# Two places of a two-layer decoder kernel in another order: the end of the linear recurrence, and the casts, sums and first products at the entries of the FFNs

## The chip, the core and the metric

The kernel runs on one core of a Trainium2 chip. The metric is device microseconds (us) of one execution, as a median over several. Three runs of the kernel before gave 2107.00, 2108.28 and 2108.45 us. A core has five engines that run side by side and wait for each other through semaphores: PE (matrix products), ACT (ScalarE), DVE (VectorE), POOL (GpSimd) and SP, whose queue issues most DMAs. PEld is PE's loading of weights. PE writes its sums to PSUM, in banks of 128 partitions by 512 floats; all else lies in SBUF.

## The reference

A decoder trunk of two layers on 1024 tokens of width 1024. Layer 0 mixes tokens by a linear recurrence with 8 heads of 128, layer 1 by attention over a sliding window of 128. Each mixer and each FFN is followed by a layer norm of alpha times the residual plus the result.

```python
q, f, i, g = jnp.split(h @ w_in, 4, axis=-1)
fg = lb + (1.0 - lb) * jax.nn.sigmoid(heads(f))
o = hgrn2_chunkwise(jax.nn.silu(heads(q)), 1.0 - fg, heads(i), jnp.log(fg))
#   S_t = diag(f_t) S_{t-1} + k_t v_t^T ; o_t = S_t^T q_t
o = o * lax.rsqrt(jnp.mean(jnp.square(o), -1, keepdims=True) + RMS_EPS)
o = o * g_norm_w * jax.nn.silu(heads(g))
mix = o.reshape(B, S, D) @ w_out

h = layer_norm(ALPHA * h + mix, ln_mix_g, ln_mix_b)
u = causal_depthwise_conv3(h @ w_in) + conv_b      # 1024 -> 2 x 2816
a, b = jnp.split(u, 2, axis=-1)
h = layer_norm(ALPHA * h + (jax.nn.silu(a) * b) @ w_out, ln_ffn_g, ln_ffn_b)
```

## The kernel before

**Numbers.** All is fp32. An operand of a product is kept as two parts: a high part, which ACT makes by a cast, and a low part, which DVE makes by subtracting the high part from the source (`split`, L197 and L249). A product then takes three matmuls, high by high (L222), high by low (L223) and low by high (L224), all written by `mm3`. `T` is the input of products, transposed, both parts; `HL` holds weights.

**Order.** The object `od` keeps a model clock: each matmul adds its time to `od.t`, and after each group of three `od.tick()` lets the generators whose time has come issue their next work on ACT and DVE. A generator's `yield 2.0` means that its next part is issued when PE's model clock is 2 us on. In the recurrence the instructions of all engines stand in exactly the order in which they were issued; in the FFN only PE's do, and a scheduler orders ACT and DVE by tiles and priority (`urgent()`). Each engine runs its own instructions in order, so one that waits holds up those behind it.

**The recurrence and its end.** The four projections (q and f as one pair for each head, i and g as another) are made by seven products p = 1 to 7 on half-size blocks (sums of blocks of the input in `Y`, `T` and `TX`), 98 steps n in the list `line`. They go to four banks of PSUM. `evacuate` empties a bank after its last product: by a copy (L1391, p = 1; L1393, L1395, L1397) or, for f (p = 4), by a tanh of the late half, after `yield 2.0` a tanh of the early half (L1403), and then `kept_back` (L1023 and L1024: the affine step for fg, and kp = 1 - fg). Beside the projections `recur` runs the recurrence of each head: products qs x kp (L1136) and qp = qs x fg (L1137), a tree over levels of block length, transposes of kp, then the state chain, St copied from the first PSUM part (L1210) and six steps (L1212). The last head, 7, is finished after the projections. The output projection (L1550, `out_pass`) covers it: `out_split` makes the parts of its weights (cast L1453, low part queued in `out_lows`), and `move` brings the normed outputs of heads 0 to 6, which were stored in HBM and come back by DMA into the tiles fg, qs, kp and Y, into `T` (cast L1470, low part queued in `moved_lows`); head 6 comes from `VG`. Head 7's output is normed in L1247 to L1266: sums of squares (sq), og, eight transposes of og (L232), gates (L1265, in four pieces), cast and low part into `T`, and it enters the last products (kc = 7).

**The entry of the FFN.** `Up` makes the first FFN product, again as seven products p on sums of blocks. `ln` takes one block of 128 rows through the layer norm (L280, L283), eight transposes on PE, and the parts. Blocks 4 to 7 are done first; for blocks tb = 0 to 3 it writes the parts of `T` and a copy `hf` of the transposed block (L437), from which, with `sf` of block tb + 4, DVE makes three sums (L447 to L449), whose parts go to `T2` (p = 7) and `TX` (p = 6 and 3). `run` first makes products 4 and 5, on blocks 4 to 7 alone, while blocks 0 to 3 are made; then 1 and 2, which read blocks 0 to 3, each with 512 columns; then 6, 7 and 3, which read the sums. `fc` is the piece of 128 outputs; `collect` takes a product out of PSUM (p = 1: two copies on ACT, L510 and L511). Products 6 use the banks of products 1 again.

Of the kernel before, what the change touches and what calls it, by code (L numbers as in the profile page):

```python
# [10 lines left out]
F32 = mybir.dt.float32  # L11
# [123 lines left out]
def trunk(ctx: ExitStack, tc: tile.TileContext, a: dict, out: bass.AP):  # L135
# [270 lines left out]
    class Up:  # L406
        def __init__(self, l, pool, rx):
            self.l, self.rx = l, rx
            self.wv = a["ffn_w_in"][l].rearrange("(kc p) c -> p kc c", p=P)
            self.TX = pool.tile([P, 2, 2, 4, 512], F32R, name="TX")  # L410
            self.T2 = pool.tile([P, 2, 4, 512], F32R, name="T2")
            self.left = None if l else pool.tile([P, 512], F32, name="lf")
            self.W, self.raw, self.pieces = {}, {}, 0

        def row_loads(self):

# [5 lines left out]
        def ln(self, tb):  # L422
            with urgent():
                ln_affine(tb, self.rows, lambda hs: ynd[:, tb, hs], 2 if tb == 3 else 1)
            yield 10.0 if tb >= 4 and self.l else 8.0 if self.l else 13.0 if tb >= 4 else 11.0
            turned = lambda t: (self.rx[2 * t - 4] if t in (2, 3) else Y[:, t, :]).rearrange("p (k t) -> p k t", k=KC)
            hf = turned(tb)
            ts = slice(tb * P, (tb + 1) * P)
            with urgent():
                for q in range(2):  # L430
                    ps, ks = psmm(), slice(4 * q, 4 * q + 4)
                    for k in range(4):
                        tr(ps[:, k * P:(k + 1) * P], Y[:, tb, (4 * q + k) * P:(4 * q + k + 1) * P])
                    pv = ps.rearrange("p (k t) -> p k t", k=4)
                    if tb < 4:
                        split(T[:, 0, ks, ts], T[:, 1, ks, ts], pv)
                        nc.scalar.copy(hf[:, ks], pv)  # L437
                    elif q == 0:
                        nc.scalar.copy(hf[:, ks], pv)
                    else:  # L440
                        split(T[:, 0, ks, ts], T[:, 1, ks, ts], pv)
                        tt(hf[:, ks], hf[:, :4], pv, op=add)
                        split(T[:, 0, :4, ts], T[:, 1, :4, ts], hf[:, ks])
                        return
            sf = turned(tb + 4)
            a11, a12, a21, s1 = hf[:, :4], hf[:, 4:], sf[:, :4], sf[:, 4:]
            tt(a21, a11, a21, op=sub)  # L447
            tt(a11, s1, a11, op=sub)
            tt(a12, a12, a11, op=sub)  # L449
            split(self.T2[:, 0, :, ts], self.T2[:, 1, :, ts], a21)  # L450
            yield 100.0
            pair = hf.rearrange("p (c k) t -> p c k t", c=2)
            split(self.TX[:, :, 0, :, ts], self.TX[:, :, 1, :, ts], pair)

        def weights(self, fc):
            self.weight_load(fc)
# [31 lines left out]
            split(blocks(1, 0), blocks(1, 1), r1)  # L488
            split(blocks(2, 0), blocks(2, 1), r2)

        def product(self, p, fc, ps):
            TX = self.TX
            moving = {1: lambda j, k: T[:, j, k, :512], 2: lambda j, k: T[:, j, 4 + k, :512],
                      3: lambda j, k: TX[:, 1, j, k, :], 4: lambda j, k: T[:, j, 4 + k, 512:],
                      5: lambda j, k: T[:, j, k, 512:], 6: lambda j, k: TX[:, 0, j, k, :],
                      7: lambda j, k: self.T2[:, j, k, :]}[p]
            block = {1: 0, 2: 1, 5: 2, 4: 3, 7: 4, 6: 5, 3: 6}[p]
            ws = self.W[fc]
            fixed = lambda j, k: (ws[6][:, 512 * j + 128 * k:512 * j + 128 * k + 128] if block == 6 else
                                  ws[block // 2 * 2 + j][:, 512 * (block % 2) + 128 * k:512 * (block % 2) + 128 * k + 128])  # L500
            for k in range(4):
                mm3(ps, lambda j: fixed(j, k), lambda j: moving(j, k), k == 0, k == 3)
                od.tick()
            return ps

# [51 lines left out]
        def run(self, ready, down):  # L557

            od.finish(ready[:4])
            tiles = [psax(), psax()]  # L560
            ax = [tiles[i % 2][:, i // 2 * 512:(i // 2 + 1) * 512] for i in range(4)]

            for (p, fc), ps in zip([(p, fc) for p in (4, 5) for fc in range(2)], ax):
                self.product(p, fc, ps)
            od.finish(ready[4:])
            mm = [psmm() for _ in range(4)]
            self.pairs = [mm, ax]
            for (p, fc), ps in zip([(p, fc) for p in (1, 2) for fc in range(2)], mm):
                self.collect(p, fc, self.product(p, fc, ps))
            for fc in range(2):  # L570
                self.collect(6, fc, self.product(6, fc, mm[fc]))
            for fc in range(2):
                self.collect(7, fc, self.product(7, fc, mm[2 + fc]))
                self.collect(4, fc, ax[fc])
                self.collect(5, fc, ax[2 + fc])
            self.weights(2)
            for fc in range(2):
                self.collect(3, fc, self.product(3, fc, mm[fc]))
            banks, n = mm[2:] + ax[:2] + mm[:2] + ax[2:], 0
            for fc in range(2, NF):  # L580
                if fc > 2:
                    self.weights(fc)
                for p in (1, 2, 6, 7, 4, 5, 3):
                    self.collect(p, fc, self.product(p, fc, banks[n % 8]))
                    n += 1
                    if fc == NF - 1 and p in (1, 6, 4):
                        down.ahead.append(down.operands(0, len(down.ahead)))
# [140 lines left out]
    with tc.tile_pool(name="t", bufs=1, reuse_waits="tile") as raws, hgrn_pool as hp:  # L728
# [323 lines left out]
        def recur(h, qs, fg, kp):  # L1052
# [80 lines left out]

            yield 0.0
            r0 = hp.tile([P, S], F32, name="St")
            nc.vector.tensor_tensor(r0, qs, kp, op=ALU.mult)  # L1136
            nc.vector.tensor_tensor(qp, qs, fg, op=ALU.mult)  # L1137
            od.vec(4.4)
            r1 = hp.tile([P, S // 2], F32, name="r1")
            nc.vector.tensor_tensor(r1, kp[:, 0::2], qp[:, 1::2], op=ALU.mult)  # L1140
            update(0)
            r2 = hp.tile([P, 2, S // 4, 2], F32, name="kd")
            for j in range(2):
                nc.vector.tensor_tensor(r2[:, j], kp[:, j::4].unsqueeze(2).to_broadcast([P, S // 4, 2]),
# [235 lines left out]
        def evacuate(m, p, ps, taken):  # L1380
# [9 lines left out]
            if p == 1:  # L1390
                nc.scalar.copy(first[:, early], ps)  # L1391
            elif p == 6:
                nc.scalar.copy(second[:, early], ps)  # L1393
            elif p == 5:
                nc.scalar.copy(second[:, late], ps)  # L1395
            elif p == 4 and g:
                nc.scalar.copy(first[:, late], ps)  # L1397
                od.spawn(turn_values(h), 3.0)
            elif p == 4:
                nc.scalar.activation(first[:, late], ps, AF.Tanh, scale=0.5)  # L1400
                taken.append(1)
                yield 2.0
                nc.scalar.activation(first[:, early], first[:, early], AF.Tanh, scale=0.5)  # L1403
                kept_back(h, first, kp, slice(0, S))
            else:
                half, to = {2: (early, first), 7: (late, second), 3: (early, second)}[p]
                tt(to[:, half], to[:, half], ps, op=add)
                od.vec(0.7)
                taken.append(1)
                yield od.behind(0.1, 0.8)  # L1410
                if p != 2:
                    nc.scalar.activation(to[:, half], to[:, half], AF.Silu)
# [38 lines left out]
        def out_split(u, place):  # L1451
# [4 lines left out]
            def low():  # L1456
                low_part(hl[:, 1], oraw[u], hl[:, 0], None)
                od.vec(1.2)
                if u == 0:
                    out_load(3)  # L1460
            out_lows.append((od.t + 1.3, low))
            yield 0.0

        def move(h0, n, half, src, wait):
# [18 lines left out]
        with tc.manual_schedule(engines={EN.PE, EN.SP, EN.Activation, EN.DVE, EN.Pool}):  # L1483
# [26 lines left out]
            for n, (m, p) in enumerate(line):  # L1510
# [2 lines left out]
                product(n)  # L1513
                opened[0] = len(line)
                h, g = pairs[m]
                if n == 90:
                    od.finish(evacs[12])
                    ready.append((NH - 1, targets[12]))
                elif n > lead and line[n - lead][1] == 4 and pairs[line[n - lead][0]][1] == 0 and n - lead < 90:
                    mr = line[n - lead][0]  # L1520
                    od.finish(evacs[mr])
                    ready.append((pairs[mr][0], targets[mr]))
                if n == 90:
                    ensure(len(line) - 1)
                if n in (91, 93, 95, 97):
                    u = (91, 93, 95, 97).index(n)
                    moved.append(od.spawn(out_split(u, (1, 2, 3, 0)[u]), 4.0 if u == 0 else 0.4))
                if n == 93:
                    Y.renew(0)
                    kept = [hp.tile([P, S], F32, name=name, bufs=b) for name, b in (("fg", 1), ("qs", 1), ("kp", 2))]  # L1530
                    halves = [[stage(t, (2 * i, 2 * i + 1), 0) for i, t in enumerate(kept)],
                              [stage(Y[:, i, :], (2 * i, 2 * i + 1), 1) for i in range(3)]]
                    moved += [od.spawn(move(2 * i, 2, 0, halves[0][i], 6.0 + 2.0 * i)) for i in range(3)]
                if n == 94:
                    moved += [od.spawn(move(2 * i, 2, 1, halves[1][i], 9.0 + 2.0 * i)) for i in range(2)]
                if n == 95:
# [392 lines left out]
```

## Time and profile before

The profiled execution took 2106.06 us; its span, from the first to the last instruction, is 2104.3 us, and all times in the views count from the span's start.

| what | value |
|---|---|
| median of three runs | 2108.28 us |
| profiled execution | 2106.06 us |
| its span | 2104.3 us |
| ACT busy in the span | 972.7 us |
| DMA, mean over the span | 136 GB/s |
| recurrence and its output projection end at about | 480 us |
| first FFN entry (products 4, 5, then 1) | 523 to 552 us |
| second FFN entry | 1466 to 1490 us |

In a row of the timeline stand start, length, engine, line, operation, output and inputs by the program's names without buffer numbers, shape and count; in brackets the idle time just ahead of it and the instruction that ended it. A matmul of 512 columns has a length of 0.39, but those that follow each other overlap in part; a row with x8 runs from the start of the first to the end of the last.

### The profile page before, as it was taken

Reading aid. Unit: us, or ns where it says so; the run is one execution under the profiler, and the core shown is the slowest. Engines: PE = TensorE matmul, PEld = TensorE weight load, DVE = VectorE, ACT = ScalarE, POOL = GpSimd, SP = SyncE. Lnnn points to the kernel's source line nnn. Section 1 sums busy time; section 2 is a strip of 40 time slices with the busy share of each in tenths; the row PEclk is TensorE's granted clock in tenths of the full one; section 3 lists DMA queues with packets and bytes.
Section 4 is the critical chain, followed back from the end, with each engine's and each line's share of the span. In section 5 each row is a group of like instructions: output and inputs, shape, how many; then the busy total and the mean of one; then the engine's idle time right before and its main releaser. Section 6 shows DMA issues by size and latency. Waiting matters only on the chain.

```text
span 2104.3 us, 31586 instructions
## 1 busy us (share of the span) xinstructions
PE 2081.6 (99%) x12303; PEld 1734.4 (82%) x12303; DVE 1775.6 (84%) x2424; ACT 972.7 (46%) x1580; POOL 176.3 (8%) x210
## 2 busy tenths in 40 slices
PE   9999999999999999999999999999999999999998
PEld 8878888778788888888888888888888888888886
DVE  6778887769999998987987678979999998978986
ACT  6555555643544444444433367733544444444430
POOL 1000000001000000000001123412000000000002
PEclk9999999999999999999999999999999999999999
DMA  4111111333256866538755411051266776459662
GB/s 154 41 51 51 51 52 51 119 118 120 84 147 176 193 163 156 136 124 299 247 184 171 140 36 46 14 174 78 87 177 171 170 190 150 116 163 323 220 217 94
DMA packets 239823, 286.82 MB, mean 136 GB/s; under 512 B 30216, under 2 KB 160440, under 8 KB 239416
## 3 DMA queue, kind: packets, MB, share of 16 engines
q1 hardware_dynamic: 223360, 238.26, 35.0%
q0 software_dynamic: 15456, 46.16, 11.0%
q8 instruction: 97, 1.59, 0.3%
q14 instruction: 54, 0.44, 0.1%
q10 hardware_dynamic: 856, 0.37, 0.1%
HBM read 241.72 MB, written 89.15 MB: 157 GB/s over the span
## 4 chain that ended last, share of the span: by engine, by line
PE 88%; DVE 7%; ACT 3%; DMA 1%; issue 1%; POOL 0%; SPq 0%; DVEq 0%; ACTq 0%; POOLq 0%
PE psmm L222 17%; PE psmm L224 17%; PE psmm L223 17%; PE psax L222 9%; PE psax L224 9%; PE psax L223 9%; PE psax L228 3%; PE psmm L228 1%; PE psax L1703 1%; PE psmm L232 1%; PE psax L232 1%; DVE HL L197 1%; DVE T L197 1%; PE psmm L1550 1%; ACT HL L1310 1%
## 5 line engine op out<-in xcount | busy, mean ns | idle before, releaser
L222 PE MATMUL psmm<-T,HL 128*128 128x512 f32 x816 | 322.5, 395 | 3.5 <-ACT T L249 2.2
L223 PE MATMUL psmm<-T,HL 128*128 128x512 f32 x816 | 318.0, 390 | 1.4 <-DVE T L197 1.4
L224 PE MATMUL psmm<-T,HL 128*128 128x512 f32 x816 | 318.1, 390 | 0.2 <-DVE HL L197 0.2
L532 DVE SCALAR_TENSOR_TENSOR Y<-Y,cwt,Y 128x1023 f32<-128x1023 f32 (+1 forms) x176 | 225.2, 1281 | 45.5 <-ACT Y L530 44.1
L249 ACT CAST HL<-rx 128x1024 fp32r<-128x1024 f32 (+1 forms) x151 | 151.4, 1007 | 184.5 <-DMA rx<-in_ffn_w_in_dram 48.5
L197 DVE TENSOR_TENSOR HL<-rx,HL 128x1024 fp32r<-128x1024 f32 (+1 forms) x151 | 174.6, 1161 | 20.9 <-ACT HL L249 20.8
L222 PEld LDWEIGHTS psmm<-T,HL 128*128 128x128 f32 x816 | 153.3, 188 | 36.0 <-ACT T L249 2.4
L224 PEld LDWEIGHTS psmm<-T,HL 128*128 128x128 f32 x816 | 153.2, 188 | 33.0 <-DVE HL L197 0.6
L223 PEld LDWEIGHTS psmm<-T,HL 128*128 128x128 f32 x816 | 153.2, 188 | 32.2 <-DVE T L197 2.1
L222 PE MATMUL psax<-T,HL 128*128 128x512 f32 x392 | 152.7, 390 | 0.0
L224 PE MATMUL psax<-T,HL 128*128 128x512 f32 x392 | 152.5, 389 | 0.0
L223 PE MATMUL psax<-T,HL 128*128 128x512 f32 x392 | 152.5, 389 | 0.0
L530 ACT ACTIVATE Y<-Y,cwt 128x1024 f32<-128x1024 f32 x88 | 108.8, 1238 | 91.7 <-DVE Y L519 86.3
L197 DVE TENSOR_TENSOR HL<-raw,HL 128x512 fp32r<-128x512 f32 (+1 forms) x121 | 92.2, 787 | 31.9 <-ACT HL L1310 22.5
L271 POOL TENSOR_TENSOR rs<-rs,nhalf 128x1 f32<-128x1 f32 x32 | 45.6, 1427 | 735.3 <-DVE rs L270 735.3
L249 ACT CAST HT<-rx 128x1024 fp32r<-128x1024 f32 (+1 forms) x37 | 35.5, 960 | 112.5 <-DVE rx L486 60.3
L222 PE MATMUL psmm<-HL 128*128 128x512 f32 x220 | 86.8, 394 | 0.0
L223 PEld LDWEIGHTS psax<-T,HL 128*128 128x128 f32 x392 | 73.7, 188 | 15.3
L222 PEld LDWEIGHTS psax<-T,HL 128*128 128x128 f32 x392 | 73.5, 188 | 15.3
L224 PEld LDWEIGHTS psax<-T,HL 128*128 128x128 f32 x392 | 73.6, 188 | 15.2
L224 PE MATMUL psmm<-HL 128*128 128x512 f32 x220 | 85.8, 390 | 0.0
L223 PE MATMUL psmm<-HL 128*128 128x512 f32 x220 | 85.6, 389 | 0.0
(406 smaller groups left out, 5177.3 us busy)
## 6 DMA issues: line engine op xcount, KB each, us to landing
rx<-in_ffn_w_in_dram SPq DMA_DIRECT2D x136, 256.0 KB
rx<-gd SPq DMA_DIRECT2D x118, 256.0 KB
bsd<-in_ffn_w_out_dram POOLq DMA_DIRECT2D x36, 768.0 KB, 8.6
gd<-Y SPq DMA_DIRECT2D x44, 512.0 KB
raw<-in_hgrn_w_in_dram SPq DMA_DIRECT2D x30, 512.0 KB
rx<-in_ffn_w_out_dram SPq DMA_DIRECT2D x54, 256.0 KB
R<-bsd SPq DMA_DIRECT2D x44, 256.0 KB
Y<-in_ffn_w_in_dram SPq DMA_DIRECT2D x40, 256.0 KB
```

The source lines that it names most:

```text
L197: make = lambda e: e.tensor_tensor(lo, src, hi.bitcast(F32), op=ALU.subtract)
L222: nc.tensor.matmul(ps, st(0), mv(0), start=start, stop=False, skip_group_check=onto)
L223: nc.tensor.matmul(ps, st(0), mv(1), start=False, stop=False, skip_group_check=onto)
L224: nc.tensor.matmul(ps, st(1), mv(0), start=False, stop=stop, skip_group_check=onto)
L228: nc.tensor.matmul(ps, lhsT, rhs, start=start, stop=stop, **kw)
L232: nc.tensor.transpose(ps, src, ident)
L249: nc.scalar.copy(hi, src)
L271: nc.gpsimd.tensor_tensor(rs, rs, nhalf, op=ALU.pow)
L530: nc.scalar.activation(c, u, AF.Identity, bias=cwt[:, l, 3, ci:ci + 1], scale=cwt[:, l, 2, ci:ci + 1])
L532: nc.vector.scalar_tensor_tensor(c[:, sh:], u[:, :S - sh], cwt[:, l, 2 - sh, ci:ci + 1], c[:, sh:], op0=ALU.mult, op1=ALU.add)
L1310: nc.scalar.copy(home(n)[:, 0], source(m, p))
L1550: nc.tensor.matmul(ps, T[:, x, kc, tb * P:(tb + 1) * P], us[kc][:, w, :], start=start and kc == 0, stop=False)
```

## The change

1. `evacuate`, p = 4: the early tanh, the affine step and kp are issued at 3.0 instead of 2.0 on the model clock.
2. `recur`: qp is made ahead of qs x kp; in head 7 another 3.0 lies between the first update and the products for `kd`.
3. Main loop: head 7's gates are finished and handed to `recur` at n = 91, not 90. The tiles for the moved heads are loaded in the order kp, qs, fg (heads 0 and 1 into kp), and their moves start at 3.0, 5.0 and 7.0, not 6.0, 8.0 and 10.0. The low part of the first output weights may go 6.0 behind its cast, not 1.3.
4. `Up.ln`, both layers: high part and copy are made by ACT one after the other, and the low part is made from the copy. The three sums are made as s1 - a11, a11 - a21 and a12 - s1, and each sum's parts directly behind it, in the order of the products that read them (6, 7, 3). The generator stops after the parts of `T` and after each sum; `make` takes all blocks to a given stage.
5. `Up.run`: blocks 0 to 3 are taken to stage 1 ahead of products 1, to stages 2, 3 and 4 behind. In layer 0 products 1 are made in two goes, 24 matmuls on the columns of blocks 0 to 2 (384), and 24 on those of block 3 (128).

```diff
@@ Up.ln
                     if tb < 4:
-                        split(T[:, 0, ks, ts], T[:, 1, ks, ts], pv)
+                        nc.scalar.copy(T[:, 0, ks, ts], pv)
                         nc.scalar.copy(hf[:, ks], pv)
+                        low_part(T[:, 1, ks, ts], hf[:, ks], T[:, 0, ks, ts], None)
...
+            self.made[tb] = 1
+            yield 100.0
             sf = turned(tb + 4)
             a11, a12, a21, s1 = hf[:, :4], hf[:, 4:], sf[:, :4], sf[:, 4:]
+            tt(s1, s1, a11, op=sub)
+            split(self.TX[:, 0, 0, :, ts], self.TX[:, 0, 1, :, ts], s1)
+            self.made[tb] = 2
+            yield 100.0
             tt(a21, a11, a21, op=sub)
-            tt(a11, s1, a11, op=sub)
-            tt(a12, a12, a11, op=sub)
             split(self.T2[:, 0, :, ts], self.T2[:, 1, :, ts], a21)
+            self.made[tb] = 3
             yield 100.0
-            pair = hf.rearrange("p (c k) t -> p c k t", c=2)
-            split(self.TX[:, :, 0, :, ts], self.TX[:, :, 1, :, ts], pair)
+            tt(a12, a12, s1, op=sub)
+            split(self.TX[:, 1, 0, :, ts], self.TX[:, 1, 1, :, ts], a12)
+            self.made[tb] = 4
+
+        def make(self, ready, part):
+            for tb, task in enumerate(ready):
+                while self.made[tb] < part:
+                    od.step(task)
@@ Up.product: a slice cols of the columns, all 512 by default
-                mm3(ps, lambda j: fixed(j, k), lambda j: moving(j, k), k == 0, k == 3)
+                mm3(ps[:, cols], lambda j: fixed(j, k), lambda j: moving(j, k)[:, cols], k == 0, k == 3, n=cols.stop - cols.start)
@@ Up.run
-            od.finish(ready[4:])
+            self.make(ready[4:], 1)
...
-            for (p, fc), ps in zip([(p, fc) for p in (1, 2) for fc in range(2)], mm):
+            firsts = list(zip([(p, fc) for p in (1, 2) for fc in range(2)], mm))
+            if self.l == 0:
+                for (p, fc), ps in firsts[:2]:
+                    self.product(p, fc, ps, slice(0, 3 * P))
+            for part in range(2, 5):
+                self.make(ready[4:], part)
+            if self.l == 0:
+                for (p, fc), ps in firsts[:2]:
+                    self.collect(p, fc, self.product(p, fc, ps, slice(3 * P, 4 * P)))
+                firsts = firsts[2:]
+            for (p, fc), ps in firsts:
                 self.collect(p, fc, self.product(p, fc, ps))
@@ recur
             r0 = hp.tile([P, S], F32, name="St")
+            nc.vector.tensor_tensor(qp, qs, fg, op=ALU.mult)
             nc.vector.tensor_tensor(r0, qs, kp, op=ALU.mult)
-            nc.vector.tensor_tensor(qp, qs, fg, op=ALU.mult)
...
             update(0)
+            if h == NH - 1:
+                yield 3.0
             r2 = hp.tile([P, 2, S // 4, 2], F32, name="kd")
@@ evacuate, p == 4
-                yield 2.0
+                yield 3.0
@@ out_split
-            out_lows.append((od.t + 1.3, low))
+            out_lows.append((od.t + (6.0 if u == 0 else 1.3), low))
@@ main loop
-                if n == 90:
+                if n == 91:
                     od.finish(evacs[12])
                     ready.append((NH - 1, targets[12]))
...
-                if n == 90:
+                if n == 91:
                     ensure(len(line) - 1)
...
-                    kept = [... for name, b in (("fg", 1), ("qs", 1), ("kp", 2))]
+                    kept = [... for name, b in (("kp", 2), ("qs", 1), ("fg", 1))]
...
-                    moved += [od.spawn(move(2 * i, 2, 0, halves[0][i], 6.0 + 2.0 * i)) for i in range(3)]
+                    moved += [od.spawn(move(2 * i, 2, 0, halves[0][i], 3.0 + 2.0 * i)) for i in range(3)]
```

Lines of the changed kernel are 20 to 24 higher than those of the same code before.

**ACT at the last gates of the recurrence** (steps n = 91 to 93; fg, kp are head 7's, sq, ss belong to head 6, VG and raw to the next evacuation and the weights). Before:

```order
L1400 ACTIVATE fg<-psmm 128x512
L1310 CAST HL<-raw_112 128x512
L1403 ACTIVATE fg<-fg 128x512
L1023 ACTIVATE fg<-fg,lbt 128x1024
L1024 ACTIVATE kp<-fg,one 128x1024
L1310 CAST HL<-raw_113 128x512 x2
L1310 CAST HL<-raw_112 128x512
L1247 ACTIVATE sq,ss<-psax 128x128 x4
L1391 COPY VG_4157<-psmm 128x512
```

Now:

```order
L1424 ACTIVATE fg<-psmm 128x512
L1334 CAST HL<-raw_112 128x512
L1271 ACTIVATE sq,ss<-psax 128x128 x4
L1334 CAST HL<-raw_113 128x512 x2
L1334 CAST HL<-raw_112 128x512
L1415 COPY VG_4133<-psmm 128x512
L1427 ACTIVATE fg<-fg 128x512
L1045 ACTIVATE fg<-fg,lbt 128x1024
L1046 ACTIVATE kp<-fg,one 128x1024
```

The copy out of PSUM has moved ahead of the early tanh, the affine step and kp.

**DVE at the last chain of the recurrence** (low parts of output weights and of moved heads, then head 7's state chain; `VG_3489` is head 6). Before:

```order
L197 TENSOR_TENSOR HL<-raw_113,HL 128x1024
L197 TENSOR_TENSOR HL<-raw_114,HL 128x1024
L197 TENSOR_TENSOR T<-fg,T 128x2x512
L197 TENSOR_TENSOR T<-VG_3489,T 128x512
L197 TENSOR_TENSOR T<-qs,T 128x2x512
L197 TENSOR_TENSOR T<-kp,T 128x2x512
L1210 COPY St<-psax 128x128
L1212 SCALAR_TENSOR_TENSOR St<-St,tot,psax 128x128 x6
```

Now:

```order
L197 TENSOR_TENSOR HL<-raw_114,HL 128x1024
L197 TENSOR_TENSOR T<-kp,T 128x2x512
L197 TENSOR_TENSOR T<-qs,T 128x2x512
L197 TENSOR_TENSOR T<-fg,T 128x2x512
L1234 COPY St<-psax 128x128
L1236 SCALAR_TENSOR_TENSOR St<-St,tot,psax 128x128 x6
L197 TENSOR_TENSOR T<-VG_3489,T 128x512
```

The low part of head 6 has moved behind the state chain, and that of the weights in raw_113 ahead of the levels of the tree that stand before these rows. On PE, six of the 18 output products that followed the state products now stand further ahead, and the eight transposes of og have six more products ahead of them, directly in front of the first product with kc = 7.

**ACT at the first FFN entry** (blocks 2 and 3 of the rows; `T` is written from the transposes in psmm, `rx` is the copy hf, `TX` and `T_4716` are the parts of the sums). Before:

```order
L249 CAST T<-psmm 128x4x128 x2
L437 COPY rx_4709<-psmm 128x512 x2
L249 CAST TX<-Y_4187 128x2x4x128
L249 CAST T_4716<-Y_4381 128x4x128 x2
L249 CAST T<-psmm 128x4x128 x2
L249 CAST HL<-rx_4710 128x512
L249 CAST TX<-Y_4187 128x2x4x128
L437 COPY rx_4711<-psmm 128x512 x2
```

Now:

```order
L436 CAST T<-psmm 128x4x128
L437 COPY rx_4709<-psmm 128x512
L436 CAST T<-psmm 128x4x128
L437 COPY rx_4709<-psmm 128x512
L249 CAST TX<-Y_4382 128x4x128
L249 CAST T_4716<-Y_4382 128x4x128 x2
L436 CAST T<-psmm 128x4x128
L437 COPY rx_4711<-psmm 128x512
```

Cast and copy of one half block now alternate, and one small TX cast stands where one of double size stood.

More of the change, by code (lines that the diff above doesn't have):

```diff
@@ L412, in __init__ @@
             self.left = None if l else pool.tile([P, 512], F32, name="lf")
-            self.W, self.raw, self.pieces = {}, {}, 0
+            self.W, self.raw, self.pieces, self.made = {}, {}, 0, [0] * 4
         def row_loads(self):
@@ L489, in weight_sums, with product @@
             split(blocks(2, 0), blocks(2, 1), r2)
-        def product(self, p, fc, ps):
+        def product(self, p, fc, ps, cols=slice(0, 512)):
             TX = self.TX
@@ L1529, in trunk @@
                     Y.renew(0)
-                    kept = [hp.tile([P, S], F32, name=name, bufs=b) for name, b in (("fg", 1), ("qs", 1), ("kp", 2))]
+                    kept = [hp.tile([P, S], F32, name=name, bufs=b) for name, b in (("kp", 2), ("qs", 1), ("fg", 1))]
                     halves = [[stage(t, (2 * i, 2 * i + 1), 0) for i, t in enumerate(kept)],
                               [stage(Y[:, i, :], (2 * i, 2 * i + 1), 1) for i in range(3)]]
-                    moved += [od.spawn(move(2 * i, 2, 0, halves[0][i], 6.0 + 2.0 * i)) for i in range(3)]
+                    moved += [od.spawn(move(2 * i, 2, 0, halves[0][i], 3.0 + 2.0 * i)) for i in range(3)]
                 if n == 94:
```

## The prediction

> **What bounds the kernel now.** I read the engine totals first, then windows of the span, then PE's own waits.
>
> ```profile
> PE 2081.6 (99%) x12303; PEld 1734.4 (82%) x12303; DVE 1775.6 (84%) x2424; ACT 972.7 (46%) x1580; POOL 176.3 (8%) x210
> 400.00:450.00 50.00, 45.95 (x487) 36.53 (x486) 38.68 (x62) 28.51 (x51) 3.02 (x2) 1.00 0.47 158
> 500.00:550.00 50.00, 46.96 (x237) 38.73 (x236) 49.57 (x81) 25.51 (x44) 8.77 (x6) 1.00 0.25 95
> 600.00:1100.00 500.00, 500.00 (x2207) 413.98 (x2207) 446.29 (x510) 212.02 (x225) 24.36 (x32) 1.00 0.66 187
> 1450.00:1500.00 50.00, 50.00 (x242) 41.84 (x241) 46.81 (x71) 23.32 (x36) 5.29 (x4) 1.00 0.25 85
> PE psmm L222 <- ACT VG L1391: 2.2, 1, 2.2
> PE psmm L222 <- ACT T L249: 2.2, 1, 2.2
> ```
>
> PE is busy 2081.6 of 2104.3 us at full clock (the 1.00 in each window row; the columns are length, then busy time and count of PE, PEld, DVE, ACT and POOL, then clock, DMA share, GB/s). All that any reordering can win is the 22.7 us that are left. Two windows hold 7.1 of them: 4.05 at the end of the recurrence (400 to 450) and 3.04 at the first layer's FFN entry (500 to 550), where DVE is full as well (49.57 of 50). From 600 to 1100, and at the second layer's entry (1450 to 1500), PE stands still nowhere, so a gain made earlier travels to the end undiminished, and a stall new there would be a pure loss. The two wait rows (total, times, longest) are PE's longest waits, one in each of these windows.
>
> **Part 1, end of the recurrence: what goes.** A matmul of 512 columns starts 0.2265 us after the one before it (the four at 425.16 below take 1.07, three steps and 0.39 for one), so the loss is the late start minus last start plus 0.2265.
>
> ```profile
> 400.97 1.24 ACT L1023 ACTIVATE fg<-fg,lbt 128x1024 f32<-128x1024 f32 x1
> 402.24 1.15 ACT L1024 ACTIVATE kp<-fg,one 128x1024 f32<-128x1024 f32 x1
> 403.30 1.64 ACT L1310 CAST HL<-raw 128x512 fp32r<-128x512 f32 x3
> 404.31 0.39 PE L224 MATMUL psmm<-T,HL 128*128 128x512 f32 x1
> 405.75 1.22 DVE L1136 TENSOR_TENSOR St<-qs,kp 128x1024 f32<-128x1024 f32 x1
> 406.31 0.58 ACT L1391 COPY VG<-psmm 128x512 f32<-128x512 f32 x1
> 406.94 0.50 PE L222 MATMUL psmm<-Y,HL 128*128 128x512 f32 x1 [2.23 <-ACT VG L1391]
> 425.16 1.07 PE L1550 MATMUL psmm<-HL,T 128*128 128x512 f32 x4
> 426.00 1.03 ACT L1470 CAST T<-kp 128x1024 fp32r<-128x1024 f32 x1
> 427.08 1.66 PE L1550 MATMUL psmm<-HL,T 128*128 128x512 f32 x6 [0.85 <-ACT T L1470]
> 433.80 1.07 PE L1550 MATMUL psmm<-HL,T 128*128 128x512 f32 x4
> 434.57 2.35 DVE L197 TENSOR_TENSOR HL<-raw,HL 128x1024 fp32r<-128x1024 f32 x2
> 435.84 2.33 PE L1550 MATMUL psmm<-HL,T 128*128 128x512 f32 x9 [0.97 <-DVE HL L197]
> ```
>
> (a) PE waits for the copy of its PSUM bank by L1391, which stands on ACT behind a tanh of 512 columns (about half an operation of 1024, 0.6), the affine step (402.24 - 400.97 = 1.27), kp (1.1), three HL casts (1.64) and four sums of squares. The change puts the copy ahead of the first three, 3.0 us, so that it ends near 403.9 and the bank is free before 404.5. Gone: 406.94 - 404.54 = 2.40. kp then is ready near 406.9, not 403.4. DVE doesn't stand still for it: qp, which needs only fg, takes the place of L1136 at 405.75 (1.22), and the product with kp follows.
> (b) The cast T<-kp is last in the queue of moved heads. The change loads kp first, fg last, and starts the moves 3 us earlier. Gone: 427.08 - (425.16 + 4 x 0.2265) = 1.01.
> (c) The HL low parts (DVE, L197) come two steps of the recurrence earlier. Gone: 435.84 - (433.80 + 0.91) = 1.13.
> Together 4.54 us. The six other heads have only the swap of two DVE products; PE has no wait there in the rows above, and I put it at 0, between -0.2 and +0.2.
>
> **Part 1: what comes.**
>
> ```profile
> 437.98 0.68 DVE L197 TENSOR_TENSOR T<-VG,T 128x512 fp32r<-128x512 f32 x1
> 441.92 1.72 PE L228 MATMUL psax<-VG,kd 128*128 128x128 f32 x14
> 443.40 3.92 PE L1550 MATMUL psmm<-HL,T 128*128 128x512 f32 x16
> 443.68 0.29 DVE L1210 COPY St<-psax 128x128 f32<-128x128 f32 x1 [2.75 <-PE psax L228]
> 444.01 2.27 DVE L1212 SCALAR_TENSOR_TENSOR St<-St,tot,psax 128x128 f32<-128x128 f32 x6
> 463.49 1.04 PE L232 MATMUL psax<-ident,og 128*128 128x128 f32 x8
> 464.57 1.27 DVE L1265 SCALAR_TENSOR_TENSOR VG<-psax,par,VG 128x256 f32<-128x256 f32 x3 [6.57 <-PE psax L232]
> 465.08 1.19 ACT L249 CAST T<-VG 128x256 fp32r<-128x256 f32 x3 [10.35 <-DVE VG L1265]
> 465.75 0.39 PE L222 MATMUL psmm<-HL,T 128*128 128x512 f32 x1
> ```
>
> (d) The low part T<-VG of head 6 (before at 437.98, ahead of the state chain) now stands on DVE behind the St copy and the six St steps, which wait for PE's VG,kd products; the lows of Y queue behind it in turn. From the start of VG,kd (441.92) the chain ends at +4.27 (444.01 + 2.27 less the overlap of 0.09) and the low at +4.95. On PE, 1.48 after that start, follow the output products; the changed order has 53 of them ahead of VG,kd, the pass with the low parts begins after 56, and its seventh needs head 6: nine more, so PE stands there at +1.48 + 9 x 0.2265 = +3.52. New wait: 1.4. Ends: 0, if DVE takes the low in its idle 2.75 after all, and 1.7 with one DVE operation more.
> (e) The transposes of og stood ahead of six products, which covered the way to DVE (464.57), ACT (465.08, 0.40 for the first of three) and back; the next product came at 465.75, 2.26 after the transposes began. Now the six stand ahead of the transposes: 1.36, then 465.48 - 463.49 = 1.99 until the first cast, 3.35 in all. New wait: 1.1 (0 to 1.4). DVE and ACT idle there, so nothing queues in front.
> Part 1: -4.54 + 1.4 + 1.1 = **-2.0**, from -4.5 to -1.4. From 465 on DVE, ACT and the DMAs hang on PE's output and shift with it.
>
> **Part 2, entry of the first FFN.**
>
> ```profile
> 539.65 1.41 DVE L283 SCALAR_TENSOR_TENSOR Y<-Y,rs,rx 128x512 f32<-128x512 f32 x2
> 541.69 1.18 ACT L437 COPY rx<-psmm 128x512 f32<-128x512 f32 x2 [3.62 <-DVE T L197]
> 542.28 1.03 PE L232 MATMUL psmm<-ident,Y 128*128 128x128 f32 x8
> 542.88 1.05 ACT L249 CAST TX<-Y 128x1024 fp32r<-128x1024 f32 x1
> 543.84 1.13 ACT L249 CAST T<-Y 128x512 fp32r<-128x512 f32 x2
> 544.88 1.06 ACT L249 CAST T<-psmm 128x512 fp32r<-128x512 f32 x2
> 545.50 0.49 PE L222 MATMUL psmm<-T,HL 128*128 128x512 f32 x1 [2.19 <-ACT T L249]
> 546.52 0.50 PE L223 MATMUL psmm<-T,HL 128*128 128x512 f32 x1 [0.52 <-DVE T L197]
> 1219.09 1.10 PE L1703 MATMUL psax<-Kh,q 128*128 128x128 f32 x8
> ```
>
> PE's transposes of the last row block end at 543.07 (eight at 0.1), and it stands until the block's casts come at 545.4, behind 2.2 us of other casts on ACT. ACT had idled 3.62 before, since its copy waited for DVE's read of the same PSUM. Changed: ACT makes T and copy at once, DVE reads the copy, and PE does 24 products of 384 columns (rows 0 to 2) while block 3 is cast. These start at 543.1; at 0.2265 x 384/512 = 0.170 each they end at 547.2. Then come 24 products of 128 columns. The nearest rows with 128x128 weights and 128 columns are the fourteen VG,kd products (441.92 to 443.40, 0.106 each) and the eight of L1703 (1.10, 0.1375 each at most); by columns alone it would be 0.2265/4 = 0.057. For all 24 the ends are 1.4 and 3.3. I take 0.110, next to the fourteen: 2.64, done at 549.9. Before, the same products were done at 551.75 (546.52 and 23 steps of 0.2265). Gain **1.8**, from 3.1 to 1.2.
> Does the data keep up? ACT casts block 3 at 545.8, so 547.2 is clear. DVE, one operation of 0.6 shorter up to L283, leaves that at 540.45; eleven half-size operations at 0.60, the low of block 3 the last, end at 547.05. The second product of the 128s wants it at 547.3. That margin of 0.3 is thin; one DVE operation more costs 0.3 to 0.6. DVE also has eight TX lows of 512 (0.60) for four of 1024 (1.13), +0.3. Later users: the second bank of product 6 comes free near 556.5 and is wanted at 558.0. I take -1.8, with 0 as the poor end.
>
> One row shows how weight loads lie beside products:
>
> ```profile
> L222 PEld LDWEIGHTS psmm<-T,HL 128*128 128x128 f32 x816 | 153.3, 188 | 36.0 <-ACT T L249 2.4
> ```
>
> A load of 0.188 for each product, all on the same 128 rows, and still a product starts each 0.2265: loads overlap products here. [...]
>
> **Part 3, entry of the second FFN.** It gets the new order of casts and sums without the split. In the window from 1450 PE has no wait. Block 3's lows come after about the same number of DVE operations as before. I put it at 0; a delay over some 2 us would be needed to show.
>
> **The rivals.**
> R1, the new waits don't come: (d) and (e) vanish behind work that the order hides, the entry gains as above. -4.5 - 1.8 = -6.3: 2102.0. For it: DVE idles 2.75 before the St copy. Against: DVE's order is fixed.
> R2, the split returns little: load and columns of the 128s add up, 0.110 + 0.057 = 0.167 each, 1.4 more for 24 and a gain of 0.4; or DVE, full there (49.57 of 50), brings block 3's low 1.8 late, and the gain is 0. With part 1 that is -2.4 to -2.0: 2106.1. Against the first: the overlap in the load row; against the second: the count of DVE operations. [...]
> R3, slower: DVE at the two entries falls behind, so that product 6 finds its bank or its TX sum not ready. In the first entry the margin is 1.5; past it each us of DVE lag is a us of PE. DVE's own surplus is 0.3, so the lag must come from the chain cast, copy, low (0.59 longer for each half block than cast and low side by side): over eight halves and two entries at most 9.4. Uncovered it gives -2.0 - 1.8 + 9.4 - 1.5 = +4.1: 2112.4. It decides from 5.3 us of lag on. Against: 1450 to 1500 shows ACT at 23.32 of 50, with room.
>
> **How the numbers follow.** The sum, -2.0 - 1.8 = -3.8, takes the profiled execution from 2106.06 (span 2104.3) to 2102.3. That execution is 2.2 below the median of the three, 2108.28; on the median's scale the forecast is **2104.5**. Forecast 0.5 (2103.0 to 2106.0), R1 0.25, R2 0.18, R3 0.07. About 0.2% (4.2 us) is what a measurement of this kernel can tell from no change; the forecast lies just inside. Faster by more: R1 and 0.18 of the forecast's 0.5, 0.43. Within: 0.32 of it, R2, and a little of R3, 0.52. Slower: 0.05. The range goes from R1 with a little more at the entry to a failed entry: 2101.4 to 2108.0.
>
> **What would show it.** PE's waits for L1391, for the casts of T<-kp and for the HL lows gone, in their place about 1.4 before the seventh product of the low pass and 1.1 behind the og transposes; PE busy near 48.7 of 50 in the stretch from 400 (idle there only 1.25, the new wait as the profile counts it). At the entry 24 products at 0.170 with no wait ahead of more than 0.1, 24 at 0.110, and no wait between. Wrong would be: a new wait after 550, or 128-column products apart by 0.17.

## The result, and the profile after

The changed kernel takes 2102.78 us (median of 11 runs, 2102.0 to 2105.73), the kernel before 2108.28 (11 runs, 2107.0 to 2111.99): ratio 0.9973, 95% interval 0.9964 to 0.9982, so some 5.5 us faster (3.8 to 7.6). Two later comparisons gave 0.9975 each (0.9966 to 0.9984, and 0.9965 to 0.9985). The forecast was 2104.5, the range 2101.4 to 2108.0. One run of the kernel before (2306.86 us) and one of `recur_only` below (3499.04) went at a far lower clock (0.85 and 0.556) and are left out of all figures.

The profiled execution took 2104.41 us (span 2102.6), only 1.65 less than that of before. This difference between profiles and medians turned out to be the point of the case.

Engine totals, windows and PE's waits of the changed kernel (columns as before):

```profile
PE 2083.4 (99%) x12327; PEld 1737.3 (83%) x12327; DVE 1773.6 (84%) x2432; ACT 970.3 (46%) x1588; POOL 174.9 (8%) x210
400.00:450.00 50.00, 48.81 (x509) 39.95 (x508) 38.73 (x62) 29.52 (x54) 1.83 (x2) 1.00 0.51 174
500.00:550.00 50.00, 49.38 (x263) 41.88 (x262) 49.10 (x81) 24.60 (x44) 8.78 (x6) 1.00 0.25 94
600.00:1100.00 500.00, 499.17 (x2202) 412.62 (x2201) 446.83 (x511) 209.60 (x224) 24.35 (x32) 1.00 0.66 187
PE psmm L1574 <- DVE T L197: 1.2, 1, 1.2
PE psmm L222 <- ACT T L249: 1.0, 1, 1.0
PE psax L222 <- DVE Y L534: 0.5, 1, 0.5
PE psax L222 <- ACT Y L523: 0.3, 1, 0.3
```

PE's idle time from 400 to 450 fell from 4.05 to 1.19, from 500 to 550 from 3.04 to 0.62, and 0.83 is new behind 600, where it had none. The waits of 2.2 us for the PSUM copy and for block 3's cast are gone. The first two waits in the list are the two that part 1 was to bring, the last two were not foreseen.

The first of these, the low part of head 6 behind the state chain (timeline: start, length, engine, line, operation, count, idle time ahead and what ended it):

```profile
438.63 1.72 PE L228 MATMUL psax<-VG,kd 128*128 128x128 f32 x14
440.11 2.33 PE L1574 MATMUL psmm<-HL,T 128*128 128x512 f32 x9
440.72 2.27 DVE L1236 SCALAR_TENSOR_TENSOR St<-St,tot,psax 128x128 f32<-128x128 f32 x6
442.90 0.68 DVE L197 TENSOR_TENSOR T<-VG,T 128x512 fp32r<-128x512 f32 x1
443.64 0.74 PE L1574 MATMUL psmm<-HL,T 128*128 128x512 f32 x2 [1.19 <-DVE T L197]
```

Nine products, then a wait for the tenth until DVE, behind six steps of the chain, has made the low part. The second, behind the og transposes:

```profile
461.68 1.04 PE L232 MATMUL psax<-ident,og 128*128 128x128 f32 x8
463.28 1.19 ACT L249 CAST T<-VG 128x256 fp32r<-128x256 f32 x3 [10.34 <-DVE VG L1289]
463.74 0.50 PE L222 MATMUL psmm<-HL,T 128*128 128x512 f32 x1 [1.01 <-ACT T L249]
```

The entry of the first FFN:

```profile
531.81 0.69 DVE L197 TENSOR_TENSOR T<-Y,T 128x512 fp32r<-128x512 f32 x1 [0.46 <-ACT Y L437]
538.08 1.40 DVE L283 SCALAR_TENSOR_TENSOR Y<-Y,rs,rx 128x512 f32<-128x512 f32 x2
540.26 1.03 PE L232 MATMUL psmm<-ident,Y 128*128 128x128 f32 x8
541.05 0.42 PE L222 MATMUL psmm<-T,HL 128*128 128x384 f32 x1
545.32 0.22 PE L222 MATMUL psmm<-T,HL 128*128 128x128 f32 x1
545.43 0.68 DVE L197 TENSOR_TENSOR T<-rx,T 128x512 fp32r<-128x512 f32 x1
546.16 0.33 PE L223 MATMUL psmm<-T,HL 128*128 128x128 f32 x1 [0.62 <-DVE T L197]
548.78 0.44 PE L222 MATMUL psmm<-T,HL 128*128 128x512 f32 x1
```

24 products of 384 columns take 4.27 (0.178 each), the 128s follow each other in 0.114 (23 steps from 546.16 to 548.78), and between them PE waits 0.62 for DVE's low part of block 3.

**Where the time went**, read as the start of one and the same PE instruction in both profiles. The changed execution was 0.56 late before it came to the change (all marks from 190 to 385 us agree in that), which is taken off in the last column.

| mark on PE | before | changed | change, start taken off |
|---|---|---|---|
| transposes of kp, head 6 | 384.76 | 385.33 | 0 |
| transposes of og, head 7 | 463.49 | 461.68 | -2.37 |
| transposes of block 3 | 542.28 | 540.26 | -2.58 |
| first matmul of product 2 | 551.86 | 548.78 | -3.64 |
| 216 matmuls later | 601.43 | 597.84 | -4.15 |
| 384 matmuls later | 639.51 | 637.35 | -2.72 |
| first score product of layer 1 | 1219.09 | 1216.94 | -2.71 |

Part 1 gives 2.4, the entry 1.1, a small wait of before (0.29 at 598.7) is gone as well; then 1.4 is given back between 619 and 634. After that PE keeps its lead, to 0.1, up to its last product; what follows that product took 0.42 longer. By the waits in these two profiles the change is worth 2.7 us; the medians say 5.5. A third profile of the changed kernel (`after_c` below) is 3.6 ahead at the last mark (1215.27, with a start 0.19 early).

### The profile page after: what moved, and what is told of

Its sections match the earlier page's. It is cut to its first block, busy times and chain, and to the rows that moved or that the text cites. A ratio compares the mean times of both kernels' runs of the same rounds, so it can differ in the third digit from the quotient of the medians.

```text
span 2102.6 us, 31643 instructions
## 1 busy us (share of the span) xinstructions
PE 2083.4 (99%) x12327; PEld 1737.3 (83%) x12327; DVE 1773.6 (84%) x2432; ACT 970.3 (46%) x1588; POOL 174.9 (8%) x210
## 4 chain that ended last, share of the span: by engine, by line
PE 89%; DVE 6%; ACT 2%; DMA 2%; issue 1%; SPq 0%; POOL 0%; DVEq 0%; ACTq 0%; POOLq 0%
PE psmm L222 17%; PE psmm L223 17%; PE psmm L224 17%; PE psax L222 9%; PE psax L223 9%; PE psax L224 9%; PE psax L228 3%; PE psmm L228 1%; PE psax L1727 1%; PE psax L232 1%; PE psmm L232 1%; DVE HL L197 1%; DMA rx<-in_ffn_w_in_dram 1%; PE psmm L1574 1%; DVE T L197 1%
## 5 line engine op out<-in xcount | busy, mean ns | idle before, releaser
L222 PE MATMUL psmm<-T,HL 128*128 128x512 f32 (+1 forms) x824 | 324.3, 394 | 1.0 <-DVE VG L1431 0.8
L223 PE MATMUL psmm<-T,HL 128*128 128x512 f32 (+1 forms) x824 | 319.8, 388 | 1.5 <-DVE T L197 1.5
L224 PE MATMUL psmm<-T,HL 128*128 128x512 f32 (+1 forms) x824 | 319.9, 388 | 0.2 <-DVE HL L197 0.2
L222 PEld LDWEIGHTS psmm<-T,HL 128*128 128x128 f32 x824 | 154.7, 188 | 32.8 <-issue 1.3
L224 PEld LDWEIGHTS psmm<-T,HL 128*128 128x128 f32 x824 | 154.8, 188 | 32.6 <-DVE HL L197 0.6
L223 PEld LDWEIGHTS psmm<-T,HL 128*128 128x128 f32 x824 | 154.9, 188 | 32.3 <-DVE T L197 2.2
```

The lines of the kernel that those rows point to most:

```text
L222: nc.tensor.matmul(ps, st(0), mv(0), start=start, stop=False, skip_group_check=onto)
L223: nc.tensor.matmul(ps, st(0), mv(1), start=False, stop=False, skip_group_check=onto)
L224: nc.tensor.matmul(ps, st(1), mv(0), start=False, stop=stop, skip_group_check=onto)
```

## The experiments

**1. The parts apart, and each kernel's profile again.** `recur_only` has the edits in `recur`, `evacuate`, `out_split` and the main loop, `entry_only` those in `Up`.

> Only the recurrence's edits (gates, order of heads and lows, yields); the FFN entry as before. Theory A (the profile tells all): PE's waits of 2.40, 1.01 and 1.13 us go, two new ones of about 1.3 and 1.1 come, so 2.2 to 2.4 us faster than before (ratio 0.9989), and the entry's waits of 2.19 and 0.52 stay as they were. Theory B (the recurrence gives more than its own waits, since what follows it shifts in a better position to the DMAs): 3.5 to 5 us faster (0.998), with waits gone that lie behind 465 us. Theory C (most of the change's gain is the entry's): at most 1.5 us faster.

2104.99 us against 2108.13 on the same chip, ratio 0.9985 (0.9976 to 0.9994): 3.1 faster, between Theories A and B.

> Only the FFN entry's edits (both layers), the recurrence as before. Theory A: first products done about 1.1 us earlier against the transposes of block 3, one wait of about 0.6 for DVE's low part of block 3, and what is gained is partly lost to PE waits between 600 and 640 us (0.3 and 0.5 seen with the whole change): 0.4 to 1.5 us faster (ratio 0.9993 to 0.9998). Theory C: 3 us faster or more (0.9985), waits between 600 and 640 absent.

2106.69, ratio 0.9993 (0.9984 to 1.0002): 1.4 faster, as in Theory A, but not clear of no change. Its only wait behind 550 that counts is 0.96, at 623, for the copy L523.

> The whole change once more, for a second profile and the sum of the two parts on one chip. Theory A: if the waits between 600 and 640 us belong to the order of work they come again at the same places and sizes; the time is the sum of recur_only and entry_only, near ratio 0.9985. If they belong to one execution (DMA arrival), they are absent or elsewhere and the time is near ratio 0.9973.

2103.14, ratio 0.9975, so 5.0 faster, where the two parts add up to 4.5. The wait at 619 comes again (0.57), the one at 634 doesn't. The first belongs to the order of work, and entry_only shows whose order:

```profile
616.35 0.62 ACT L249 CAST HT<-rx 128x512 fp32r<-128x512 f32 x1 [5.03 <-DMA rx<-in_ffn_w_in_dram]
616.88 1.06 ACT L547 ACTIVATE Y<-Y 128x1024 f32<-128x1024 f32 x1
617.84 1.23 ACT L542 ACTIVATE Y<-Y,cwt 128x1024 f32<-128x1024 f32 x1
618.97 0.56 ACT L522 COPY Y<-psax 128x512 f32<-128x512 f32 x1
620.07 0.50 PE L222 MATMUL psax<-T,HL 128*128 128x512 f32 x1 [0.30 <-ACT Y L523]
```

In these rows of the changed kernel ACT stands 5.03 for the DMA of a weight block, and two activations and the copies that free PE's bank queue behind its cast. In the kernel before that cast stands behind the copies (row 625.15, ended by a DMA of the same tensor), and PE doesn't wait there:

```profile
615.96 0.59 ACT L511 COPY Y<-psax 128x512 f32<-128x512 f32 x1
625.15 0.62 ACT L249 CAST HT<-rx 128x512 fp32r<-128x512 f32 x1 [0.53 <-DMA rx<-in_ffn_w_in_dram]
```

> The kernel before, for a second profile. If the profile of before was typical, PE's waits are the same to 0.1 us each (sum 14.8 us) and the span is near 2104; if executions differ, some wait not in the first profile shows up, of 1 to 3 us, or the clock is lower.

2109.21 us, span 2107.3, with the same waits on PE (14.4 us in all). By the marks it is 0.65 late from the start on, and 3.05 late at 1219. The other 2.4 come in one place, behind the wait for block 3's cast; the last column but two of a window row is the granted clock:

```profile
545.98 0.79 PE L222 MATMUL psmm<-T,HL 128*128 128x512 f32 x1 [2.20 <-ACT T L249]
547.59 0.63 PE L224 MATMUL psmm<-T,HL 128*128 128x512 f32 x1
548.02 0.63 PE L222 MATMUL psmm<-T,HL 128*128 128x512 f32 x1
547.00:553.00 6.00, 6.00 (x15) 4.75 (x16) 6.00 (x10) 4.01 (x6) 0.00 (x0) 0.53 0.01 4
```

Matmuls start every 0.43 instead of 0.23. The profile of entry_only has such a stretch too (clock 0.93 from 400 to 410), behind the other long wait, 2.23 at 405; it cost 1.6 (11 steps from 408.32 to 412.43, 4.11 us for 2.49). The first profiles of both kernels have none, and for the kernel before that was not typical. The mean granted clock of each run tells how often it happens: in 16 of 80 timed runs of the kernel before it was 0.999 (not 1: behind PE's last products the clock fell too, to 0.69 from 2100 to 2104 in the first profile of before), in the others 0.998 to 0.996; of the changed kernel in 28 of 30. recur_only and entry_only, which have one wait of 2.2 us each, have 2 of 10 and 3 of 11.

In the first profile of before PE stood 2.23 ahead of 406.94 and 2.19 ahead of 545.50, and the clock behind both was 1.00 (from 407 to 417 and from 546 to 556). In before_again the same two waits were there, and half clock followed the second, of 2.20, with another 0.22 one matmul later. So a wait of 2.2 us was followed by half clock in one execution and not in another of the same kernel. What decides it isn't shown.

**2. Is it the idle PE, and what are the pieces worth?** `gates_only` is the kernel before with this edit (the condition on n stands in two places):

```diff
-                yield 2.0
+                yield 3.0
...
-                if n == 90:
+                if n == 91:
```

> The kernel before with the gates alone moved (3.0 for 2.0 in evacuate, n == 91 for n == 90). Theory W (only waits count): PE's wait of 2.23 for the bank goes, the waits of 0.85 and 0.97 stay or grow a little, 1.5 to 2.4 us faster than before. Theory C (a PE wait of 2.2 us is in some executions followed by a stretch at half clock, which costs 1.8 to 2.4 us more; seen in two profiles, 1.9 and 3.6 us behind such a wait): the mean granted clock over the runs rises from 0.9978 (before) to about 0.9982 as in recur_only, since only the entry's wait is left, and the time falls by 2.5 to 3.3 us, more than the wait itself.

2107.72, ratio 0.9997 (0.9988 to 1.0006): nothing, against both theories. The wait for the bank is gone, and comes back in two pieces:

```profile
406.90 1.23 DVE L1136 TENSOR_TENSOR St<-qs,kp 128x1024 f32<-128x1024 f32 x1 [2.62 <-ACT kp L1024]
414.90 1.09 PE L232 MATMUL psax<-ident,og 128*128 128x128 f32 x8 [1.33 <-DVE og L1251]
417.61 0.50 PE L222 MATMUL psmm<-Y,HL 128*128 128x512 f32 x1 [1.62 <-ACT VG L1395]
```

kp comes late, DVE's first product waits for it, and og and the next bank's copy are late by that, with a half-clock stretch behind them (the matmuls at 418.28 and 418.70 are 0.42 apart; such a stretch cost 1.6 in entry_only). So the moved gates alone don't pay. In recur_only, which has the swap of qp and the 3.0 ahead of `kd` as well, both of these waits are absent; neither edit was run by itself. `nosplit` is the whole change without the two column slices:

```diff
-            if self.l == 0:
+            if False:
                 for (p, fc), ps in firsts[:2]:
...
-            if self.l == 0:
+            if False:
                 for (p, fc), ps in firsts[:2]:
```

> The whole change, but the first products of layer 0 in 512 columns at once. PE then waits behind the transposes of block 3 for that block's cast and low: from 541.05 until about 544.9 and again to 546.2, 3.5 to 4.8 us in all, and the first products end 546.2 + 5.2 = 551.4 instead of 548.8: 2.6 us slower than the whole change by waits alone (ratio to before about 0.9987). Theory C adds: the wait is the longest in the kernel, so most executions show a half-clock stretch behind it, the mean clock falls to 0.998 or below from 0.9989, and the time is 4 to 5 us above the whole change, about 2107.5. Theory W: clock stays 0.9989, 2105.6.

2105.21, ratio 0.9986 (0.9977 to 0.9994), 2.4 above the whole change, and no run at 0.999: mean clock 0.9975. PE in this kernel's timeline and window:

```profile
542.80 0.50 PE L222 MATMUL psmm<-T,HL 128*128 128x512 f32 x1 [2.90 <-ACT T L436]
544.08 0.50 PE L223 MATMUL psmm<-T,HL 128*128 128x512 f32 x1 [0.77 <-DVE T L197]
545.41 0.63 PE L224 MATMUL psmm<-T,HL 128*128 128x512 f32 x1
545.00:550.00 5.00, 5.00 (x17) 3.98 (x16) 3.62 (x7) 2.41 (x6) 0.00 (x0) 0.68 0.37 108
```

Two waits of 3.67 in all, and the clock falls, as in Theory C; the time comes out near Theory W's 2105.6, but not by its sum. For by the marks nosplit, less its half-clock stretch (1.6: nine steps from 544.64 to 548.29, 3.65 for 2.04), is as far ahead at 1219 as the whole change in its first two profiles: -1.1 - 1.6 = -2.7 against -2.7 (-3.6 in after_c). The loss by waits that both theories put at 2.6 isn't there: what the split saves in waits, it pays in narrow products (24 x (0.114 - 0.057) = 1.4) and in the waits at 619 and 634, which nosplit has not. By these profiles the split's gain is the clock; the runs of the next experiment bear that out in part.

`nosplit_fill` puts useless work in that wait, ahead of the first products:

```diff
+            if self.l == 0:
+                for k in range(4):
+                    mm3(mm[2], lambda j: T[:, j, k, 512:512 + P], lambda j: T[:, j, k, 512:], k == 0, k == 3)
```

> nosplit with twelve added products (2.7 us of PE, on blocks 4 to 7, into the bank of product 2 fc 0, which overwrites them) in the place of its 2.9 us wait behind the transposes of block 3; nothing becomes ready earlier by them. Theory W (only the wait counts): time as nosplit, 2105.2, or up to 0.5 slower. Theory C (the idle PE sets off the half-clock stretch): the stretch is gone, mean clock over the runs back from 0.9975 to 0.9988 or more, and the time falls by 1.7 to 2.4 us to 2103, that of the whole change, although PE does useless work.

The wait of 2.90 is filled (0.77 remains), and the profile has no half-clock stretch:

```profile
500.00:550.00 50.00, 49.23 (x245) 40.90 (x244) 49.71 (x82) 26.24 (x48) 8.16 (x6) 1.00 0.25 92
```

7 of 11 runs are at 0.999 (nosplit: none), mean clock 0.9986, in between the values of nosplit and of the whole change. The time is 2104.27, 0.9 less, where 1.7 to 2.4 was expected; the intervals of the two overlap. nosplit ran on another chip, but the kernel before had a mean clock of 0.9979 and 0.9978 on the two. The seven runs at 0.999 average 2104.1, those of the whole change (28) 2103.1: some 1 us of the split's 2.4 seems not to be the clock. That the half clock goes with an idle PE is shown by the clock of the runs (0.9975 without the added products, 0.9986 with them); its price in time is borne out in sign only. `before_fill`, nine such products in the kernel before:

> The kernel before with nine such added products (2.0 us) in its 2.19 us wait at the first FFN entry; the wait at the recurrence's end stays. Theory W: time as before, 2108.1, or up to 0.5 slower. Theory C: mean clock over the runs rises from 0.9978 to about 0.9983 (as entry_only, which also has the recurrence's wait alone) and the time falls by 0.5 to 1.5 us.

Clock up to 0.9984, 4 of 11 at 0.999; 2107.38 against 2108.43, ratio 0.9995 (0.9986 to 1.0004). As expected by the clock, within noise by the time.

**3. Without the two new waits.** `fix_de` is the whole change with the low part of head 6 issued ahead of the state chain, and head 7's norm earlier:

```diff
             St = hp.tile([P, NB, P], F32, name="St")
+            if h == NH - 1:
+                moved_lows.pop(0)[1]()
...
-            yield 5.4
+            yield 3.0 if h == NH - 1 else 5.4
```

> The whole change with its two new waits taken out again: the low part of head 6 issued on DVE ahead of the state chain, and head 7's norm 2.4 earlier on the model clock, which puts six products back behind the og transposes. Both waits are gone from PE's list (1.19 and 1.01 us), nothing else is late: 2.2 to 2.5 us faster than the whole change, median 2100.5, ratio to before 0.9963. Rival: the entry, where DVE is full, swallows it (DVE doesn't come earlier), then under 1 us faster with the wait for block 3's low part (0.62) longer by the rest.

2100.34 (5 runs), ratio 0.9961 (0.9949 to 0.9974), all at 0.999. PE has no wait left from 430 to 480; DVE makes the low part in the time it stood idle:

```profile
436.09 0.68 DVE L197 TENSOR_TENSOR T<-VG,T 128x512 fp32r<-128x512 f32 x1
439.69 0.29 DVE L1236 COPY St<-psax 128x128 f32<-128x128 f32 x1 [2.91 <-PE psax L228]
```

Once more, beside the whole change on one chip:

> fix_de once more beside the whole change on one chip. If the two new waits were the change's own loss: again near 2100.5, 2.2 to 2.5 us under the whole change, all runs at clock 0.999. If the first five runs were lucky: within 1 us of the whole change.

> The whole change beside fix_de_b: near 2103.0 as in its 22 runs so far, mean clock 0.9988 to 0.999.

2099.74 (ratio 0.9957, 0.9943 to 0.9971) and 2103.16 (0.9975): 3.4 apart, with no run of the one as slow as any of the other, and more than the 2.2 of the two waits; on different chips it was 2.4. Where the rest comes from isn't shown. It beats both kernels. What remains at the entry's aftermath in fix_de_b is 1.13, the wait for L523 again, now longer.

## Why the prediction was right, and where it was not

- **The bound.** Right for PE. Wrong was "a gain made earlier travels to the end undiminished": it was read from windows of the kernel before, but the entry's edits reorder ACT and DVE up to 640 us as well, and 1.4 went there. R3 had such a loss, for DVE and product 6; it came a few products later, on ACT behind a weight DMA (0.30) and on DVE (L534, 0.53). "A new wait after 550" stood among the signs of being wrong, and here it was.
- **Part 1, what goes (a, b, c).** Right: all three waits are gone.
- **Part 1, what comes (d, e).** Forecast 1.4 and 1.1, measured 1.19 and 1.01 as idle time (the 1.4 was to show as 1.25). R1, that they don't come, fell. The sum of part 1 was -2.0; by the marks -2.4.
- **Part 2.** Mis-sized: 1.8 forecast, 1.1 measured at product 2, 0.1 net at 639 (-2.72 against -2.58). The narrow products came as taken (0.114 for 0.110), the 384s at 0.178 for 0.170. The term that failed is DVE's lead: it was to leave L283 0.6 earlier against PE by having one operation less, but at the mark PE was 2.0 ahead and DVE's L283 only 1.6 (538.08 for 539.65). So DVE was 1.0 later against PE than worked out, and the thin margin of 0.3 became a wait of 0.62. 0.46 of it is in the row at 531.81: the low part is made from the copy now, and DVE stood that long for the copy (L437). This is the chain cast, copy, low of R3, at a twentieth of its 9.4.
- **R2's first case**, load and columns of the 128s one after the other, would have had a 128-column product take 0.167; no run shows that, 0.114 was measured. The 0.110 in that sum is the distance of products, not a load: with the 0.188 of the load row it would have been 0.245, further off still.
- **Part 3.** Right: no wait in the second entry.
- **The sum.** -3.8 forecast for -5.5 measured: the time came into the range partly by luck. It lies nearer R1's 2102.0 than the forecast, though R1's mechanism fell, and the addends were off: the waits give 2.7, not 3.8, in the first two profiles (3.6 in after_c). What the prediction didn't have is the clock: half-clock stretches that cost 1.6 to 2.4 us followed the waits of 2.2 us in most executions (64 of 80 timed runs of the kernel before have a mean clock under 0.999), and the profile it was worked from happened to have none. The row 1.00 in each window was taken for a property of the kernel; it was one of that execution.
- **How much the clock is worth** stays open between 1 and 2 us. By the mean clocks, 0.99785 before and 0.9989 after, the kernel before spent some 4.4 us more at half clock, which with a matmul each 0.43 for 0.23 would be 2.1 (an estimate). But its 16 runs at 0.999 average 2107.6 and the changed kernel's 28 such runs 2103.1: 4.4 of the 5.2 us between the averages of all 80 and 30 runs is there at the same clock. So the clock isn't all that parts profiles and medians. The profile of before, 2106.06, was faster than all 91 timed runs, and that of the changed kernel, 2104.41, slower than 9 of 11, so that the two side by side show too little. That the profile was 2.2 under the median was noted, and not asked after. How the gain divides between the two places stays open as well: by the marks at 1219, less the stretch, recur_only is worth 2.8 and entry_only 0.3, by the medians 3.1 and 1.4, each with an interval of 1.9 to either side.

## What to carry to other kernels

Compare the profiled execution with the median before working from it: where they differ by as much as the effect that is looked for, look at the granted clock of the runs, compare runs of the same clock, and profile the kernel again. Long waits of a nearly saturated PE cost more than their length here, in some executions (2.20 in before_again, and 2.4 at half rate behind it); cut the longest ones first, even into several short ones, but far apart: 1.2 and 1.0, some 20 us apart, went with no loss of clock in the changed kernel's first profile, 1.33 and 1.62 within 4 us did not in that of gates_only. And a step that is moved may need its followers moved: the gates alone gained nothing.

## What the runs showed of the hardware

Waits of 2.2 us of one core's PE were followed by matmuls at half rate in some executions and not in others of the same kernel: 0.43 for 0.23 in before_again, with a clock of 0.53 from 547 to 553, and a clock of 1.00 behind the waits of 2.23 and 2.19 in the first profile of before. Waits of 1.33 and 1.62 within 4 us were followed by it too (0.42 in gates_only), waits of 1.19 and 1.01 some 20 us apart were not (1.00 in the changed kernel). Filling a wait of 2.90 with products that nobody reads (nosplit_fill) went with 7 of 11 runs at 0.999, where nosplit had none of 11, without anything being ready earlier.
